# Token-to-channel turns by transfers of 32-partition squares and full-width transposes, and weight parts made 2048 elements at a time, in a float32 hybrid decoder layer

## The chip, the cores and the metric

The kernel runs on one core of one Trainium2 chip, in one launch. The metric is device time in microseconds (us). Engines: PE is TensorE (matmul), PEld its weight load, DVE is VectorE, ACT is ScalarE, POOL is GpSimd, SP is SyncE, which here only issues transfers. "Partition" is one of the 128 rows of on-chip memory.

## The reference

One decoder layer on x [256 tokens, 2048 channels], all float32, and a final norm:

```
h    = rmsnorm(x, ln1_w)
proj = h @ w_in          # q | k | v | pool input | z | x,B,C | dt | 3 gates: 13856 columns
att  = sliding-window attention with sinks      (1024 wide)
pool = trailing means over 2, 4, 8, 16 tokens minus the token, a map per group, a scale (1024)
ssm  = Mamba-2 SSD with conv, then y * silu(z) under a norm per group of 512   (2048)
merged = sum over the branches of sigmoid(gate_b) * (branch_b @ w_b)
x    = x + merged @ w_out
h2   = rmsnorm(x, ln2_w)
x    = x + (silu(h2 @ Wg) * (h2 @ Wu)) @ w_down     # feed-forward, 5632 wide
out  = rmsnorm(x, final_w)
```

## The kernel before, in words

Every large product is made of float32 numbers split in two parts of the type float32r, a = hi + lo, and takes three matmuls (hi hi, hi lo, lo hi; `three`, L180 to L184) into one accumulator. Weights stream from HBM in pieces of [128, n, columns], at most 2048 elements a partition, that is 1 MB: `weights` (L144) has SP load a piece into one of four `raw` buffers, and then, for each half of the piece, has ACT copy the high part into a `whi` buffer and DVE subtract it into a `wlo` buffer (`split`, L138 and L139; five buffers of 1024 elements of each). `tokens_block` (L186) is [256 tokens, up to 512 columns] = a^T W, with one accumulator per 128 tokens; `channels_block` (L210) is the product with channels on partitions. A piece of 512 columns is 24 matmuls.

The stages, in order: v and dt as x comes in; k and q; the convolutions and the attention between them; the SSD scan; the attention branch; pooling and its branch; z with the group norm of the SSD output; the SSD branch; the output projection; the feed-forward in three parts of 4, 4 and 3 blocks of 512 columns, each part's down projection behind it.

A product contracts over channels, so its left side must have channels on partitions, while a `tokens_block` leaves tokens on partitions. `turn` (L305) makes the change for a block [128 tokens, 2, 512 channels]: 16 DVE transposes (L314), each of one 32 by 32 square position over a tile of 32 partitions and 256 elements, in two groups of eight; then ACT and DVE split the result (L316 to L322; where a weight of the norm goes in, in four pieces with a scale per partition). It is used for 4 blocks of y (SSD output), 4 of m (merged), 4 of x2 (the residual) and 11 of ff (feed-forward).

Small work such as this is put in a list (`later`, `pause`) and taken from it by `side` (L122), one task for each half piece of a large product, with a share of DVE's time counted (SHARE, 1.4 us for a half piece of 1024 elements, capped at 4.0). That gives the order in which the program is written; the framework then plans each engine's own order of instructions from it by when it expects data and buffers. An engine runs its instructions in that planned order and waits at the first whose input is missing. Each transfer is queued on the engine that issues it: SP has the weights, x, the norm weights and the output; POOL has the small vectors at the start (L253, L355 to L359) and, later, a few additions (L638, L661, L703, L740).

Tiles of 4 KB a partition (`k4`) share 22 buffers.

Of the kernel before, what the change touches and what calls it, by code (L numbers as in the profile page):

```python
# [16 lines left out]
P = 128  # L17
D = 2048
# [25 lines left out]
SHARE = 1.4 / 1024  # of the vector engine's time per column of weights, for small work  # L44
# [3 lines left out]
# the constants' array: an identity, then the rest by column  # L48
# [8 lines left out]
def constants():  # L57
    c = np.zeros((P, K_N), np.float32)
    r = np.arange(P)
    c[:, K_LE:K_LE + P] = r[:, None] <= r[None, :]  # L60
    c[:, K_GT:K_GT + P] = r[:, None] > r[None, :]
    # a query's row: the previous block's keys, then its own block's
    c[:, K_MC:K_MC + P] = np.where(r[None, :] > r[:, None], 0.0, NEG)
    c[:, K_MP:K_MP + P] = np.where(r[None, :] <= r[:, None], 0.0, NEG)
    for g, w in enumerate(POOL_WINDOWS):
        n = np.minimum(np.arange(PADW) + 1, w).astype(np.float32)
        c[:, K_IV + g * PADW:K_IV + (g + 1) * PADW] = np.float32(1.0) / n
    return np.concatenate([np.eye(P, dtype=np.float32), c], axis=1)
# [3 lines left out]
def hybrid_block(ctx: ExitStack, tc: tile.TileContext, ins, out):  # L72
# [39 lines left out]
    # a task and its time on the vector engine, which is shared out over the pieces  # L112
# [22 lines left out]
    def split(src, hi, lo, scale=None):  # L135
        """src (SBUF or PSUM), times a scalar per partition, into its parts."""
        if scale is None:
            act.copy(hi, src)  # L138
            dve.tensor_tensor(lo, src, hi.bitcast(F32), ALU.subtract)  # L139
        else:  # L140
            act.activation(hi, src, AF.Copy, scale=scale)  # L141
            dve.scalar_tensor_tensor(lo, src, scale, hi.bitcast(F32), ALU.mult, ALU.subtract)

    def weights(loads, shape):  # L144
        """A piece of weights [128, n, cols], n * cols <= 2048: pairs of parts, each of half of n."""
        raw = wpool.tile([P, *shape], F32, tag="raw", name="raw", bufs=4)
        for to, src in loads:
            sp.dma_start(to(raw), src)
        n, cols = shape
        parts = []  # L150
        for h in range(2):
            a, b = h * (n // 2), (h + 1) * (n // 2)
            hi = wpool.tile([P, b - a, cols], F32R, tag="whi", name="whi", bufs=5)
            lo = wpool.tile([P, b - a, cols], F32R, tag="wlo", name="wlo", bufs=5)
            split(raw[:, a:b], hi, lo)
            parts.append((a, b, hi, lo))
        return parts
# [3 lines left out]

    class Parts:
        """An activation, channels on partitions: [128, channel tiles, 256 tokens] in two parts."""
# [16 lines left out]
    def three(o, xh, xl, yh, yl, first, last):  # L180
        """o (+)= x^T y without the product of the two low parts."""
# [4 lines left out]
    def tokens_block(a, nk, loads_of, cols, loaded=None):  # L186
        """[tokens, cols] = a^T W over nk channel tiles: one accumulator per 128 tokens."""
        accs = [acc() for _ in range(T)]
        step = 8 if cols <= 256 else 4
        for i in range(0, nk, step):  # L190
            n = min(step, nk - i)
            pieces = weights(loads_of(i, n), [n, cols])
            if loaded is not None:
                loaded(i)
            for s, e, hi, lo in pieces:
                for t in range(T):
                    tok = slice(t * P, (t + 1) * P)
                    for j in range(e - s):
                        k = i + s + j
# [9 lines left out]

    def channels_block(a, loads_of):  # L210
        """[256 channels, tokens] = W^T a over all of D: one accumulator per 128 channels."""
        accs = [acc() for _ in range(2)]
        for i in range(0, KD, 8):
            for s, e, hi, lo in weights(loads_of(i), [8, 256]):
                for j in range(e - s):
                    k = i + s + j
# [16 lines left out]
    def keep_warm(n):  # L233
        """Work for the tensor engine while it waits, so that its clock is up when the data comes."""
# [11 lines left out]
    for name, n in (("ln2_w", 16), ("ssm_norm_w", 16), ("pool_scale", 8), ("conv_b", 24)):  # L246
        VEC[name] = r0, n
        r0 += n
# [10 lines left out]
    # the engine's table, before its time  # L259
# [15 lines left out]
    def rsqrt(ss, n, shape, name, more=EPS):  # L275
        """(ss / n + more) ** -0.5: the engine's root, then a Newton step."""
# [11 lines left out]
    def transposed(block, k0, dst, scale=None):  # L288
        """block [128 tokens, 2, 512 channels] into dst's channel tiles k0..k0+3."""
# [15 lines left out]
    def turn(block, k0, dst, scale=None):  # L305
        """As transposed, by the vector engine's 32 by 32 squares: in three steps."""
        tt = k4([4, SEQ], F32, "tt")
        src = block.rearrange("p t (k j c) -> p t k j c", k=4, j=4)
        to = tt.rearrange("p k (t i s) -> p t k i s", t=T, i=4)

        def squares(rows_):
            for i in rows_:
                for j in range(4):
                    dve.transpose(to[32 * j:32 * j + 32, :, :, i, :], src[32 * i:32 * i + 32, :, :, j, :])  # L314

        def parts():  # L316
            if scale is None:
# [6 lines left out]
        later(lambda: squares((0, 1)), 2.0)  # L324
        later(lambda: squares((2, 3)), 2.0)
        later(parts, 1.2)

# [25 lines left out]
    for name in ("ln2_w", "ssm_norm_w", "pool_scale", "conv_b"):  # L353
        vec_load(name)
    pool.dma_start(vec[:96, 1, :], ins["conv_w"][0].rearrange("k (a c) -> (k a) c", c=P))  # L355
# [27 lines left out]
    # the factors as a row, on every partition  # L383
# [16 lines left out]
    # softplus(x) = max(x, 0) + 2 atanh(e / (2 + e)), e = exp(-|x|)  # L400
# [35 lines left out]
    def times_sums():  # L436
        # sums over a chunk: up to a token (second chunk), and behind it (first chunk)
# [19 lines left out]
    # ---- q and k: heads on partitions, a pair by tile; a key head in both halves of its tile  # L457
# [17 lines left out]
    def att_scores(j):  # L475
        for n in range(T):
# [6 lines left out]
            # the heads of one half of the partitions to a bank  # L483
# [73 lines left out]
    def conv(a, ci, dst):  # L557
        """Causal convolution and SiLU of a channel tile: a [128, 256] in PSUM."""
# [18 lines left out]
    # decay, and the product of C and B, by chunk and group  # L577
# [15 lines left out]
    def mix_product(c, g):  # L593
        """[s, 8 heads, l]: (C_l . B_s) exp(sum over s < t <= l of dt a), zero for s > l."""
# [15 lines left out]
    # B of the first chunk, tokens on partitions  # L610
# [22 lines left out]
    def ssd_x(c, g):  # L633
# [3 lines left out]
        # the skip term, in place  # L637
# [56 lines left out]
    def branch(br, j, a_parts, w, sg):  # L694
# [3 lines left out]
        for t, a in enumerate(tokens_block(a_parts, nk, plain_loads(w, 0, j * NB, NB), NB)):  # L698
# [15 lines left out]
    po = Parts(8, "po")  # L714

    def pool_mix(pair):
# [3 lines left out]
        for (g, mhi, mlo), (_, _, wh, wl) in zip(pair, w2):  # L720
# [44 lines left out]
    ssg = tiny([T, GROUPS], "ssg", 1)  # L765
    ssm = Parts(KD, "ssm")
    for g in range(GROUPS):
# [13 lines left out]
        turn(ys[g], 4 * g, ssm, lambda k: vcol("ssm_norm_w", k))  # L781
# [3 lines left out]
    for j in range(4):  # L785
# [7 lines left out]
        elif j > 1:  # L793
            turn(m4[j], 4 * j, mp)

# [8 lines left out]
    for j in range(4):  # L804
        for t, a in enumerate(tokens_block(mp, KD, plain_loads(ins["w_out"][0], 0, j * NB, NB), NB)):
# [3 lines left out]
        turn(x2[j], 4 * j, x2p, lambda k: vcol("ln2_w", k))  # L809
# [11 lines left out]
    def down(j, c0, cols, i, accs):  # L821
        """A block's sums into the residual; where i is given, they are whole."""
# [11 lines left out]
    for some in FF_PARTS:  # L834
        f = Parts(4 * len(some), "f")
        for i, b in enumerate(some):
            a_ = k4([T, NB], F32, "ff")
            for t, a in enumerate(tokens_block(x2p, KD, plain_loads(wgu, 0, b * NB, NB), NB)):
                act.activation(a_[:, t, :], a, AF.Silu, scale=rstd2[:, t:t + 1])
            if b == FB - 1:  # L840
                # the root's table, before its time
                act.activation(tiny([1], "junk1"), a_[:, 1, :1], AF.Square)
                act.activation(tiny([1], "junk1"), rstd2[:, :1], AF.Sqrt)
            for t, a in enumerate(tokens_block(x2p, KD, plain_loads(wgu, 0, DFF + b * NB, NB), NB)):
# [3 lines left out]
            turn(a_, 4 * i, f)  # L848
        k0, nk = 4 * some[0], 4 * len(some)
        last = some[-1] == FB - 1  # L850
        for j in range(3 if last else 4):
            down(j, 0, NB, j if last else None, tokens_block(f, nk, plain_loads(wd, k0, j * NB, NB), NB))
    down(3, 0, 256, 3, tokens_block(f, nk, plain_loads(wd, k0, 3 * NB, 256), 256))

# [1 line left out]
    wl = []  # L856
    for i in range(0, nk, 8):
        n = min(8, nk - i)
        raw = wpool.tile([P, n, 256], F32, tag="raw", name="raw", bufs=4)
        sp.dma_start(raw, rows(wd, k0 + i, n, 3 * NB + 256, 256))  # L860
# [55 lines left out]
```

## Time and profile before

| | |
|---|---|
| median of 3 runs | 1677.84 us (1677.47 to 1678.03) |
| span of the profiled execution, first to last instruction | 1675.7 us |
| that execution's time outside its span | not shown; the median lies 2.1 us above the span |
| PE, PEld busy | 1660.0 us (99%), 1417.6 us (85%) |
| DVE, ACT, POOL busy | 1145.6 us (68%), 792.7 us (47%), 61.1 us (4%) |
| moved by DMA | 312.5 MB, 184468 packets, 187 GB/s in the mean |

A timeline row has start (us from the span's first instruction), duration in us, engine, line of the kernel, operation, output<-inputs, shape, count, and in brackets the engine's idle time before it and what ended that. Matmuls overlap: a row of 0.39 us may be followed by the next 0.23 us later, so starts are compared, not durations. A row of groups has the busy us and the mean ns of one instruction behind the first bar, and the idle time before them behind the second.

### The profile page before, as it was taken

What the parts mean: (1) busy time and instruction counts of PE and PEld (TensorE: products, weight loads), DVE (VectorE), ACT (ScalarE), POOL (GpSimd) and SP (SyncE); (2) the same over time, 40 slices, a digit from 0 to 9 for tenths busy, and PEclk for the clock granted to TensorE, in tenths of its full rate; (3) what the DMA queues carried; (4) which work ended last, traced back from release to release, by engine and by line L of the source; (5) the groups of instructions that cost most, each with busy time, mean ns of one, the idle gap of its engine ahead of it and who ended that gap; (6) DMA issues with size and microseconds to landing.
All of it is one profiled execution on the core that took longest, in us unless ns stands there. A gap on an engine that the chain in (4) does not pass through costs nothing.

```text
span 1675.7 us, 21335 instructions
## 1 busy us (share of the span) xinstructions
PE 1660.0 (99%) x8511; PEld 1417.6 (85%) x8511; DVE 1145.6 (68%) x1577; ACT 792.7 (47%) x970; POOL 61.1 (4%) x53
## 2 busy tenths in 40 slices
PE   9999999999999999999999999999999999999997
PEld 8999998888988888888788888888888888888887
DVE  7688788885654469945798866665456666546675
ACT  6357555444444457644445544443344444344443
POOL 1000001110220000000000000000000000000000
PEclk9999999999999999999999999999999999999999
DMA  9544454455566555566475565556565556555552
GB/s 295 183 150 155 153 191 151 151 165 163 160 218 200 185 193 193 185 202 199 152 250 185 178 211 185 195 201 212 191 200 192 187 199 197 186 194 201 186 178 88
DMA packets 184468, 312.53 MB, mean 187 GB/s; under 512 B 7388, under 2 KB 57824, under 8 KB 184368
## 3 DMA queue, kind: packets, MB, share of 16 engines
q1 hardware_dynamic: 183856, 310.67, 56.5%
q8 instruction: 66, 1.08, 0.3%
q0 software_dynamic: 368, 0.43, 0.1%
q14 instruction: 34, 0.28, 0.0%
q10 hardware_dynamic: 144, 0.07, 0.0%
HBM read 309.05 MB, written 2.10 MB: 186 GB/s over the span
## 4 chain that ended last, share of the span: by engine, by line
PE 93%; DVE 4%; ACT 1%; DMA 1%; issue 1%; SPq 0%; DVEq 0%; ACTq 0%
PE acc L184 30%; PE acc L182 30%; PE acc L183 30%; DVE wlo L139 1%; DVE tt L314 1%; PE sm L644 1%; DMA x<-in_x_dram 1%; PE tr L489 1%; ACT whi L138 0%; DVE cv L565 0%; PE sm L604 0%; PE sm L532 0%; PE tr L521 0%; DVE y L631 0%; PE sm L651 0%
## 5 line engine op out<-in xcount | busy, mean ns | idle before, releaser
L139 DVE TENSOR_TENSOR wlo<-raw,whi 128x1024 fp32r<-128x1024 f32 (+2 forms) x582 | 705.4, 1227 | 454.3 <-ACT whi L138 453.1
L138 ACT CAST whi<-raw 128x1024 fp32r<-128x1024 f32 (+2 forms) x582 | 603.6, 1040 | 741.4 <-PE acc L184 622.5
L183 PE MATMUL acc<-wlo,x2p_hi 128*128 128x512 f32 x704 | 274.0, 389 | 0.0
L184 PE MATMUL acc<-whi,x2p_lo 128*128 128x512 f32 x704 | 274.0, 389 | 0.0
L182 PE MATMUL acc<-whi,x2p_hi 128*128 128x512 f32 x704 | 274.0, 389 | 0.0
L182 PE MATMUL acc<-whi,h_hi 128*128 128x512 f32 (+1 forms) x544 | 212.7, 392 | 1.0 <-ACT h_hi L141 1.0
L183 PE MATMUL acc<-wlo,h_hi 128*128 128x512 f32 (+1 forms) x544 | 208.8, 384 | 0.3 <-DVE wlo L139 0.3
L184 PE MATMUL acc<-whi,h_lo 128*128 128x512 f32 (+1 forms) x544 | 208.7, 385 | 0.3
L182 PE MATMUL acc<-h_hi,whi 128*128 128x256 f32 x672 | 191.6, 285 | 0.0
L184 PE MATMUL acc<-h_hi,wlo 128*128 128x256 f32 x672 | 190.7, 284 | 0.0
L183 PE MATMUL acc<-h_lo,whi 128*128 128x256 f32 x672 | 190.7, 284 | 0.0
L183 PEld LDWEIGHTS acc<-wlo,x2p_hi 128*128 128x128 f32 x704 | 132.2, 188 | 27.4
L184 PEld LDWEIGHTS acc<-whi,x2p_lo 128*128 128x128 f32 x704 | 132.2, 188 | 27.4
L182 PEld LDWEIGHTS acc<-whi,x2p_hi 128*128 128x128 f32 x704 | 132.2, 188 | 27.4
L184 PE MATMUL acc<-whi,f_lo 128*128 128x512 f32 (+1 forms) x352 | 134.6, 382 | 0.4 <-DVE f_lo L139 0.4
L182 PE MATMUL acc<-whi,f_hi 128*128 128x512 f32 (+1 forms) x352 | 134.5, 382 | 0.0
L183 PE MATMUL acc<-wlo,f_hi 128*128 128x512 f32 (+1 forms) x352 | 134.5, 382 | 0.0
L182 PEld LDWEIGHTS acc<-h_hi,whi 128*128 128x128 f32 x672 | 128.9, 192 | 2.1 <-issue 1.5
L184 PEld LDWEIGHTS acc<-h_hi,wlo 128*128 128x128 f32 x672 | 128.9, 192 | 1.4 <-issue 1.3
L183 PEld LDWEIGHTS acc<-h_lo,whi 128*128 128x128 f32 x672 | 128.9, 192 | 0.4 <-issue 0.3
L182 PEld LDWEIGHTS acc<-whi,h_hi 128*128 128x128 f32 x544 | 102.1, 188 | 23.2 <-issue 1.9
L183 PEld LDWEIGHTS acc<-wlo,h_hi 128*128 128x128 f32 x544 | 102.2, 188 | 22.2 <-issue 1.9
(236 smaller groups left out, 1898.5 us busy)
## 6 DMA issues: line engine op xcount, KB each, us to landing
raw<-in_w_in_dram SPq DMA_DIRECT2D x106, 1024.0 KB, 5.2
raw<-in_w_gate_up_dram SPq DMA_DIRECT2D x88, 1024.0 KB, 5.1
raw<-in_w_down_dram SPq DMA_DIRECT2D x43, 1024.0 KB, 5.2
raw<-in_w_ssm_br_dram SPq DMA_DIRECT2D x16, 1024.0 KB, 5.2
raw<-in_w_out_dram SPq DMA_DIRECT2D x16, 1024.0 KB, 5.9
raw<-in_w_attn_br_dram SPq DMA_DIRECT2D x8, 1024.0 KB, 5.1
raw<-in_w_pool_br_dram SPq DMA_DIRECT2D x8, 1024.0 KB, 5.1
x<-in_x_dram SPq DMA_DIRECT2D x8, 512.0 KB, 7.8
```

The lines of the kernel that those rows point to most:

```text
L138: act.copy(hi, src)
L139: dve.tensor_tensor(lo, src, hi.bitcast(F32), ALU.subtract)
L182: pe.matmul(o, lhsT=xh, rhs=yh, start=first, stop=False)
L183: pe.matmul(o, lhsT=xh, rhs=yl, start=False, stop=False)
L184: pe.matmul(o, lhsT=xl, rhs=yh, start=False, stop=last)
L314: dve.transpose(to[32 * j:32 * j + 32, :, :, i, :], src[32 * i:32 * i + 32, :, :, j, :])
L489: pe.matmul(p[:, i * w:(i + 1) * w], lhsT=qT[2 * j + i][half, n * P:(n + 1) * P], rhs=kT[j][half, keys], start=True, stop=True,)
L644: pe.matmul(p[:, i * HD:(i + 1) * HD], lhsT=mt[:, i, :], rhs=xdt[:, i, :], start=True, stop=True)
```

## The change

`turn` sends the block's 16 squares of 32 partitions (32 tokens, all of the two token blocks, 128 channels; 32 KB each) by 16 transfers from SBUF to SBUF into a new tile `mid`, and then makes two DVE transposes over all 128 partitions and 512 elements. The transfers are queued on POOL, or, for the last turn before its consumer (`soon`: m of the last branch block, x2 of the last block, the last ff block of each feed-forward part), on POOL, SP and ACT in rotation (6, 5, 5). The task list has the move, then a pause of 6.0 us (3.0 if soon) and then the transposes and the split in one task of 2.6. In the turned tile, partition p has channels 4p to 4p+3 of a block of 512, where it had p, p+128, p+256, p+384: so the weights of the products that read turned tiles (w_ssm_br, w_out, w_gate_up, w_down) are loaded in the matching order (`turned`, four neighbouring rows to a partition; packets as long as before), and the norm weights ln2_w and ssm_norm_w come as a [128, 4, 4] tile by two POOL transfers of runs of 4 elements, instead of rows that PE turns.

`weights` splits a whole piece at once: one ACT copy and one DVE subtraction of 2048 elements instead of two of 1024. `raw` has 3 buffers instead of 4; `whi` and `wlo` have 3 of 2048 elements instead of 5 of 1024. Comments are left out in the new file.

```diff
     def weights(loads, shape):
-        raw = wpool.tile([P, *shape], F32, tag="raw", name="raw", bufs=4)
+        raw = wpool.tile([P, *shape], F32, tag="raw", name="raw", bufs=3)
         for to, src in loads:
             sp.dma_start(to(raw), src)
-        n, cols = shape
-        parts = []
-        for h in range(2):
-            a, b = h * (n // 2), (h + 1) * (n // 2)
-            hi = wpool.tile([P, b - a, cols], F32R, tag="whi", name="whi", bufs=5)
-            lo = wpool.tile([P, b - a, cols], F32R, tag="wlo", name="wlo", bufs=5)
-            split(raw[:, a:b], hi, lo)
-            parts.append((a, b, hi, lo))
-        return parts
+        hi = wpool.tile([P, *shape], F32R, tag="whi", name="whi", bufs=3)
+        lo = wpool.tile([P, *shape], F32R, tag="wlo", name="wlo", bufs=3)
+        split(raw, hi, lo)
+        return hi, lo
+    def turned(w, k0, n, c0, cols):
+        return [
+            ((lambda r, b=b: r[:, b:b + 4, :]),
+             w[(k0 + b) * P:(k0 + b + 4) * P, c0:c0 + cols].rearrange("(p k) c -> p k c", k=4))
+            for b in range(0, n, 4)
+        ]
...
-    def turn(block, k0, dst, scale=None):
-        tt = k4([4, SEQ], F32, "tt")
-        src = block.rearrange("p t (k j c) -> p t k j c", k=4, j=4)
-        to = tt.rearrange("p k (t i s) -> p t k i s", t=T, i=4)
-        def squares(rows_):
-            for i in rows_:
-                for j in range(4):
-                    dve.transpose(to[32 * j:32 * j + 32, :, :, i, :], src[32 * i:32 * i + 32, :, :, j, :])
+    def turn(block, k0, dst, scale=None, soon=False):
+        mid = k4([T, 4, P], F32, "mid")
+        queues = (pool, sp, act) if soon else (pool,)
+        def move():
+            for n in range(16):
+                i, j = n // 4, n % 4
+                queues[n % len(queues)].dma_start(
+                    mid[32 * j:32 * j + 32, :, i, :], block[32 * i:32 * i + 32, :, j * P:(j + 1) * P]
+                )
         def parts():
+            tt = k4([4, SEQ], F32, "tt")
+            for t in range(T):
+                dve.transpose(
+                    tt.rearrange("p k (t i s) -> p t i k s", t=T, i=4)[:, t],
+                    mid[:, t].rearrange("p i (c k) -> p i k c", k=4),
+                )
...
-        later(lambda: squares((0, 1)), 2.0)
-        later(lambda: squares((2, 3)), 2.0)
-        later(parts, 1.2)
+        later(move)
+        pause(3.0 if soon else 6.0)
+        later(parts, 2.6)
...
-    for name in ("ln2_w", "ssm_norm_w", "pool_scale", "conv_b"):
+    for name in ("pool_scale", "conv_b"):
         vec_load(name)
+    vec_t = const.tile([P, 2, KD // 4, 4], F32, name="vec_t")
+    for i, name in enumerate(("ln2_w", "ssm_norm_w")):
+        pool.dma_start(vec_t[:, i], ins[name][0].rearrange("(b p k) -> p b k", p=P, k=4))
...
-            turn(m4[j], 4 * j, mp)
+            turn(m4[j], 4 * j, mp, soon=j == 3)
...
-        turn(x2[j], 4 * j, x2p, lambda k: vcol("ln2_w", k))
+        turn(x2[j], 4 * j, x2p, lambda k: tcol(0, k), soon=j == 3)
...
-            turn(a_, 4 * i, f)
+            turn(a_, 4 * i, f, soon=i == len(some) - 1)
```

## Rows read from the trace of the kernel before

**Rows 1.** The page: busy time of each engine, and the chain by engine

```profile
PE 1660.0 (99%) x8511; PEld 1417.6 (85%) x8511; DVE 1145.6 (68%) x1577; ACT 792.7 (47%) x970; POOL 61.1 (4%) x53
...
PE 93%; DVE 4%; ACT 1%; DMA 1%; issue 1%; SPq 0%; DVEq 0%; ACTq 0%
```

**Rows 2.** Stretches: busy us and instructions of each engine, PEclk, DMA share, GB/s

```profile
0.00:40.00 40.00, 36.44 (x247) 34.11 (x248) 28.07 (x66) 27.19 (x49) 5.85 (x15) 1.00 1.00 307
...
90.00:190.00 100.00, 99.72 (x799) 92.71 (x798) 82.74 (x151) 64.50 (x136) 0.00 (x0) 1.00 0.49 154
190.00:240.00 50.00, 49.24 (x407) 48.78 (x407) 46.63 (x74) 27.99 (x37) 2.44 (x2) 1.00 0.52 164
...
820.00:840.00 20.00, 17.90 (x73) 14.32 (x72) 19.46 (x29) 8.59 (x9) 1.07 (x1) 0.91 0.46 148
...
1050.00:1600.00 550.00, 550.00 (x2429) 455.57 (x2428) 329.84 (x372) 232.91 (x231) 0.00 (x0) 1.00 0.59 195
1600.00:1640.00 40.00, 39.58 (x175) 32.44 (x174) 31.41 (x46) 19.53 (x25) 0.00 (x0) 1.00 0.53 172
```

**Rows 3.** Timeline of PE, 826 to 836 us

```profile
828.94 0.39 PE L182 MATMUL acc<-whi,ssm_hi 128*128 128x512 f32 x1
831.43 0.50 PE L183 MATMUL acc<-wlo,ssm_hi 128*128 128x512 f32 x1 [2.10 <-DVE wlo L139]
...
835.65 0.39 PE L182 MATMUL acc<-whi,ssm_hi 128*128 128x512 f32 x1
```

**Rows 4.** Timeline of DVE, 770 to 850 us

```profile
812.33 7.17 DVE L314 STREAM_TRANSPOSE tt<-m 32x256 f32<-32x256 f32 x16
...
822.94 7.18 DVE L314 STREAM_TRANSPOSE tt<-m 32x256 f32<-32x256 f32 x16
```

**Rows 5.** Groups of DVE by line and shape

```profile
L139 DVE TENSOR_TENSOR wlo<-raw,whi 128x1024 fp32r<-128x1024 f32 x568 | 695.5, 1239 | 449.7 <-ACT whi L138 448.6
L314 DVE STREAM_TRANSPOSE tt<-ff 32x256 f32<-32x256 f32 x176 | 76.7, 436 | 2.6
...
L139 DVE TENSOR_TENSOR wlo<-raw,whi 128x512 fp32r<-128x512 f32 x6 | 4.0, 688 | 3.9 <-ACT whi L138 3.9
```

**Rows 6.** Groups of ACT by line and shape

```profile
L138 ACT CAST whi<-raw 128x1024 fp32r<-128x1024 f32 x568 | 594.7, 1050 | 735.9 <-PE acc L184 620.5 <-PE acc L183 90.2 <-DVE wlo L139 10.2
...
L138 ACT CAST whi<-raw 128x576 fp32r<-128x576 f32 x8 | 5.3, 670 | 0.1
```

**Rows 7.** Timeline of DVE, 1250 to 1264 us

```profile
1251.54 1.40 DVE L845 SCALAR_TENSOR_TENSOR ff<-acc,rs_r,ff 128x512 f32<-128x512 f32 x2
1252.98 7.18 DVE L314 STREAM_TRANSPOSE tt<-ff 32x256 f32<-32x256 f32 x16
```

**Rows 8.** Groups of POOL

```profile
L357 POOL DMA_DIRECT2D heads<-in_d_skip_dram x1 | 0.5, 547 | 0.0
L358 POOL DMA_DIRECT2D sink<-in_attn_sink_dram x1 | 0.5, 539 | 1.2 <-DMA vec<-in_ln_w_dram 1.2
```

**Rows 9.** Transfers: issues, size, median us to landing

```profile
raw<-in_w_gate_up_dram SPq DMA_DIRECT2D x88, 1024.0 KB, 5.1
...
out_dram<-x SPq DMA_DIRECT2D x8, 256.0 KB, 2.6
...
cst<-in_cst_dram POOLq DMA_DIRECT2D x1, 288.0 KB, 6.5
```

**Rows 10.** Timeline of DVE, then of PE, 1599 to 1613 us

```profile
1601.14 7.19 DVE L314 STREAM_TRANSPOSE tt<-ff 32x256 f32<-32x256 f32 x16
...
1611.91 0.50 PE L184 MATMUL acc<-whi,f_lo 128*128 128x512 f32 x1 [0.42 <-DVE f_lo L139]
```

**Rows 11.** Timeline of PE, from the start

```profile
9.87 0.53 PE L182 MATMUL acc<-whi,h_hi 128*128 128x288 f32 x2
```

**Rows 12.** Timeline of DVE, then of PE, 196 to 262 us

```profile
212.83 4.63 DVE L139 TENSOR_TENSOR wlo<-raw,whi 128x1024 fp32r<-128x1024 f32 x4
...
214.84 0.28 PE L184 MATMUL acc<-h_hi,wlo 128*128 128x256 f32 x1
```

More of the change, by code (lines that the diff above doesn't have):

```diff
@@ L191, in tokens_block @@
             n = min(step, nk - i)
-            pieces = weights(loads_of(i, n), [n, cols])
+            hi, lo = weights(loads_of(i, n), [n, cols])
             if loaded is not None:
                 loaded(i)
-            for s, e, hi, lo in pieces:
+            for s, e in ((0, n // 2), (n // 2, n)):
                 for t in range(T):
                     tok = slice(t * P, (t + 1) * P)
-                    for j in range(e - s):
-                        k = i + s + j
+                    for j in range(s, e):
+                        k = i + j
                         three(
@@ L208, in plain_loads, with turned_loads @@
         return lambda i, n: [(lambda r: r[:, :, :], rows(w, k0 + i, n, c0, cols))]
+    def turned_loads(w, k0, c0, cols):
+        return lambda i, n: turned(w, k0 + i, n, c0, cols)
     def channels_block(a, loads_of):
@@ L213, in channels_block @@
         for i in range(0, KD, 8):
-            for s, e, hi, lo in weights(loads_of(i), [8, 256]):
-                for j in range(e - s):
-                    k = i + s + j
+            hi, lo = weights(loads_of(i), [8, 256])
+            for s, e in ((0, 4), (4, 8)):
+                for j in range(s, e):
+                    k = i + j
                     for c in range(2):
@@ L245, in hybrid_block @@
     VEC = {}
-    for name, n in (("ln2_w", 16), ("ssm_norm_w", 16), ("pool_scale", 8), ("conv_b", 24)):
+    for name, n in (("pool_scale", 8), ("conv_b", 24)):
         VEC[name] = r0, n
@@ L351, in hybrid_block, with tcol @@
     rst = const.tile([P, SEQ], F32, name="rst")
-    for name in ("ln2_w", "ssm_norm_w", "pool_scale", "conv_b"):
+    for name in ("pool_scale", "conv_b"):
         vec_load(name)
+    vec_t = const.tile([P, 2, KD // 4, 4], F32, name="vec_t")
+    for i, name in enumerate(("ln2_w", "ssm_norm_w")):
+        pool.dma_start(vec_t[:, i], ins[name][0].rearrange("(b p k) -> p b k", p=P, k=4))
+    def tcol(i, k):
+        return vec_t[:, i, k // 4, k % 4:k % 4 + 1]
     pool.dma_start(vec[:96, 1, :], ins["conv_w"][0].rearrange("k (a c) -> (k a) c", c=P))
@@ L697, in branch @@
         nk = w.shape[0] // P
-        for t, a in enumerate(tokens_block(a_parts, nk, plain_loads(w, 0, j * NB, NB), NB)):
+        loads = turned_loads if br == 2 else plain_loads
+        for t, a in enumerate(tokens_block(a_parts, nk, loads(w, 0, j * NB, NB), NB)):
             if br == 0:
@@ L719, in pool_mix @@
         w2 = weights([(lambda r: r[:, :, :], pw[:, 2 * g0:2 * g0 + 4])], [4, 256])
-        for (g, mhi, mlo), (_, _, wh, wl) in zip(pair, w2):
+        for i, (g, mhi, mlo) in enumerate(pair):
+            wh, wl = (w[:, 2 * i:2 * i + 2] for w in w2)
             p = sm().rearrange("p (k s) -> p k s", k=2)
@@ L780, in hybrid_block @@
         later(finish, 1.5)
-        turn(ys[g], 4 * g, ssm, lambda k: vcol("ssm_norm_w", k))
+        turn(ys[g], 4 * g, ssm, lambda k: tcol(1, k))
     sg_ssm = [gate(2, j) for j in range(2)]
@@ L804, in hybrid_block @@
     for j in range(4):
-        for t, a in enumerate(tokens_block(mp, KD, plain_loads(ins["w_out"][0], 0, j * NB, NB), NB)):
+        for t, a in enumerate(tokens_block(mp, KD, turned_loads(ins["w_out"][0], 0, j * NB, NB), NB)):
             dve.tensor_tensor(x2[j][:, t, :], a, x2[j][:, t, :], ALU.add)
@@ L837, in hybrid_block @@
             a_ = k4([T, NB], F32, "ff")
-            for t, a in enumerate(tokens_block(x2p, KD, plain_loads(wgu, 0, b * NB, NB), NB)):
+            for t, a in enumerate(tokens_block(x2p, KD, turned_loads(wgu, 0, b * NB, NB), NB)):
                 act.activation(a_[:, t, :], a, AF.Silu, scale=rstd2[:, t:t + 1])
@@ L843, in hybrid_block @@
                 act.activation(tiny([1], "junk1"), rstd2[:, :1], AF.Sqrt)
-            for t, a in enumerate(tokens_block(x2p, KD, plain_loads(wgu, 0, DFF + b * NB, NB), NB)):
+            for t, a in enumerate(tokens_block(x2p, KD, turned_loads(wgu, 0, DFF + b * NB, NB), NB)):
                 dve.scalar_tensor_tensor(
@@ L851, in hybrid_block @@
         for j in range(3 if last else 4):
-            down(j, 0, NB, j if last else None, tokens_block(f, nk, plain_loads(wd, k0, j * NB, NB), NB))
-    down(3, 0, 256, 3, tokens_block(f, nk, plain_loads(wd, k0, 3 * NB, 256), 256))
+            down(j, 0, NB, j if last else None, tokens_block(f, nk, turned_loads(wd, k0, j * NB, NB), NB))
+    down(3, 0, 256, 3, tokens_block(f, nk, turned_loads(wd, k0, 3 * NB, 256), 256))
     wl = []
@@ L858, in hybrid_block @@
         n = min(8, nk - i)
-        raw = wpool.tile([P, n, 256], F32, tag="raw", name="raw", bufs=4)
-        sp.dma_start(raw, rows(wd, k0 + i, n, 3 * NB + 256, 256))
+        raw = wpool.tile([P, n, 256], F32, tag="raw", name="raw", bufs=3)
+        for to, src in turned(wd, k0 + i, n, 3 * NB + 256, 256):
+            sp.dma_start(to(raw), src)
         for b in range(0, n, 4):
```

## The prediction

> **What bounds the kernel now.** I read the page first: PE is busy 1660.0 of 1675.7 us, DVE 1145.6, ACT 792.7, POOL 61.1, and the chain that ended last is PE for 93% and DVE for 4% [rows 1]. That doesn't yet say that PE can't be fed better, so I read PE's busy time stretch by stretch: from 1050 to 1600 us it has 550.00 of 550.00 [rows 2], 2429 matmuls at 0.2264 us each. There no work taken off DVE or ACT can be worth anything. What is lost elsewhere is little [rows 2]: 3.56 us in the first 40, 0.28 from 90 to 190, 0.76 from 190 to 240, 2.10 from 820 to 840, 0.42 from 1600 to 1640. The change adds and removes no large matmul, so it lives within these few microseconds on the good side, and on the bad side in what it can make PE wait for.
>
> The one real hole is at 828.9 us: PE waits 2.10 us for a `wlo` [rows 3], and the granted clock of 820 to 840 is 0.91 where it is 1.00 in the other stretches [rows 2]. From 828.94 to 835.65 there are twelve starts; at 0.2264 us they take 2.72, so 4.0 us are lost there, wait and lower clock (1.2 instead of 2.4 GHz for part of it) together. The cause stands in DVE's timeline: two turns of m behind each other, 7.17 and 7.18 us of squares [rows 4], with hardly a weight subtraction between.
>
> **The change part by part.**
>
> *Squares on DVE go.* 23 turns of 16 transposes at 436 ns [rows 5] are 160.4 us of DVE. In their place come 46 transposes of 512 elements. None is in the trace; the nearest row is a subtraction of 512 elements, 688 ns [rows 5], so 0.70 each, 32 us in all (at twice that, 64). DVE loses about 128 us. In the feed-forward that is worth nothing: DVE goes away for 1.40 + 7.18 us at a turn [rows 7] and PE still has 550.00 of 550.00. At 828.9 it removes the cause: two turns then hold DVE for about 2.8 us of transposes, not 14.4. I take the 4.0 us as gained. What is late next there is the squares' landing, which nothing needs for more than a block.
>
> *The transfers.* A turn has 16 of 32 KB. POOL issues one in 0.547 us, and its ninth at the start of the kernel waited 1.2 us for the landing of its first [rows 8]: eight in flight. Landing takes between 2.6 us (256 KB out) and 6.5 us (a POOL transfer while the DMA engines were full) [rows 9]. With 18 turns on POOL alone: the last square issues at 8 x 0.547 + the wait + 8 x 0.547, so at 8.75 to 11.4 us after the block is done, and lands at 11 to 18. Those blocks are wanted 20 us or more later (a further block of 16 channel tiles is 96 matmuls, 21.7 us), so PE pays nothing as long as DVE does not stand waiting (the first rival). In all 12.1 MB more go over engines that are 59% busy in the long stretch [rows 2], 3.9% on 312.5 MB: hidden; if that cover were gone it would be the weights' landing, 5.1 us [rows 9], that grows, against 16.3 us which three `raw` buffers allow.
>
> The Trainium skill speaks against such transfers: DMA: Bandwidth & Descriptors, Anatomy of one DMA and Rules for kernel authors, gives each about 2.0 us fixed and says that below 64 KB one pays mostly overhead. One after the other the sixteen would by an estimate from that page take 33 us a turn. The trace has POOL issue the next before the last has landed [rows 8], so I keep 11 to 18.
>
> *The soon turns.* Five turns put 6 on POOL, 5 each on SP and ACT: 6 x 0.547 + 2.6 to 6.5 = 5.9 to 9.8 us, then 1.4 of transposes, so 7.3 to 11.2 where squares took 7.2. Behind come, as before, a high and a low part (1.05 and 1.24 us, [rows 5, 6]). Four of the five are wanted in the fourth piece of their consumer, 72 matmuls or 16.3 us after the block: 11 to 15 us is in time. The last feed-forward part has three blocks, its third piece comes at 10.9 us, and there the old turn was already late: 7.19 us of squares and a wait of PE for f_lo of 0.42 [rows 10]. The new one is 0.1 to 4.0 later unless PE is given other matmuls first. I take +1.0, ends -0.4 and +4.0. SP's own five stand in front of weight loads and wait for the block; the weights in `raw` cover that, and ACT's five cost it some 2 us of its slack.
>
> *Whole pieces.* 284 pairs of splits become single ones. By the slope between 512 and 1024 elements [rows 5] DVE takes 2.34 us instead of 2.48, by 576 and 1024 [rows 6] ACT 1.92 instead of 2.10: 40 and 51 us less in all, hidden under PE. But the first half of a piece is ready (2.34 - 1.24) + (1.92 - 1.05) = 2.0 us later, and buffers come free by the piece. So DVE may be away less long: 8.6 us cost nothing before [rows 7], about 6.6 after. Where DVE is the tight engine that shows. From 190 to 240 us it is busy 46.6 of 50 [rows 2]; at 212.83 it makes four halves in a row, each done within 1.2 us, and PE takes the first at 214.84 [rows 12]. As a whole piece it is done at about 215.2: 0.3 late, likewise for its neighbours. I take +0.5, ends -0.8 (the stretch's idle time goes) and +3. From 90 to 190 (DVE 82.7 of 100) I take 0, ends -0.3 and +2.
>
> *The start.* PE begins the products at 9.87 us [rows 11], behind a split of 576 elements, now 1152: 0.5 us later on ACT (0.67 to 1.16 by the slope), 0.6 on DVE. The DMA engines are full there, 1.00 over 40 us at 307 GB/s [rows 2]. The third `raw` buffer as the last leaves 576 KB of weights behind x, 1.9 us earlier at that rate; the two norm weights come in 1024 runs of 16 bytes, not shown in the trace, between 0 and, at the mean price of a packet (195 GB/s at 0.59 busy and 1.7 KB make 82 ns), 5.3 us on 16 engines. A packet a hundredth as long should be near the low end. I take +0.6 for all of it, ends -1.9 and +6.
>
> *The sum*, against the profiled span of 1675.7: -4.0 + 1.0 + 0.5 + 0 + 0.6 = -1.9, so 1673.8; the median of the runs lies 2.1 above the span, so **1675.9 us**. A median tells 0.2% from no change, 3.4 us here, so this is no change.
>
> **The rivals.**
>
> *A. DVE waits for the squares (slower).* DVE runs its list in order; behind the transposes stand the next weight subtractions, and PE waits for those. The point that decides is 6.6 us of standing, as above. The pause of 6.0 is 3 to 5 half pieces of 2.7 us, 8 to 14 us after the move; squares that land at 11 to 18 let DVE stand 0 to 10. For it: the landing while weights stream is not in the trace. Against it: the planner places the transposes by when it expects `mid`. Standing 7.9 us costs 1.3 at each of 18 turns: +23, some 1699 us. On the same side the Trainium skill (SBUF — State Buffer, Two separate sides) has POOL unable to write a transfer's descriptors while DVE runs a two-port operation; no run here shows it.
>
> *B. Whole pieces starve PE wherever DVE is tight (slower).* Four attention heads and four SSD groups at 1 us each beside the sum's +0.5: -1.9 + 7.5, 1683.4. For it [rows 12]; against it the stretch has only 0.76 us idle, and DVE gains 0.14 a piece.
>
> *C. The hole at 828.9 stays*, because ACT and DVE still take two turns there at once, or the landing is in the way: -1.9 + 4.0, 1679.9. So the change wouldn't do what it says for the time. Against it: 14.4 us of squares are the whole cause.
>
> *D. All holes close*: -4.0 - 0.4 - 0.8 - 0.3 - 1.0 at the start, 1671.3. For it: planner and DVE have more room everywhere. Against it: the 2.0 us of later halves.
>
> **How the numbers follow.** The sum's case has 0.55 (own range 1673 to 1679), C 0.13, D 0.12, A 0.08, B 0.12. Of the sum's 0.55 the part below 1674.5 (gain over 0.2%) is 0.23, with D 0.35 faster; the rest and C are 0.45 within 0.2%; A and B are 0.20 slower. The range runs from 1671.5 (D) to 1686 (past B), leaving out A and the edges.
>
> **What would show it.** Right: PE busy all of 820 to 840 at clock 1.00; DVE's busy time near 978 us, ACT's near 742, POOL's near 235 (318 issues of 0.547); 46 transposes near 0.70 us; no wait of DVE for `mid` over 6 us. Wrong: PE waiting for `wlo` behind a DVE that waits for a transfer (A), or in many places between 90 and 400 us (B); first products well after 10.5 us; PE waiting for f_hi or f_lo of the last part by more than 4 us.

## The result, and the profile after

The changed kernel takes 1688.59 us (median of 4 runs, 1688.1 to 1691.4) beside 1677.65 of the kernel before (4 runs, 1675.75 to 1678.03): ratio of the runs' means 1.0071, 95% interval 1.0058 to 1.0083. It is slower by 0.7%. The forecast was 1675.9, no change, with a range from 1671.5 to 1686: wrong, the measured time lies above the range.

The page after, to hold beside [rows 1]: DVE has lost 152 us, ACT 53, and the span has grown from 1675.7 to 1686.7. The chain of the page is followed back only to 897.9 us here (its shares add up to 46%, before to 100%), so the two rows can't be set side by side share by share. In the part that it covers, transfers (`mid`) and the DVE work behind them stand between the stretches of PE at x2 and in the last feed-forward part.

```profile
PE 1663.3 (99%) x8511; PEld 1417.0 (84%) x8511; DVE 993.7 (59%) x964; ACT 739.6 (44%) x679; POOL 221.1 (13%) x371
...
PE 41%; DMA 2%; DVE 2%; issue 1%; POOL 0%; ACTq 0%; DVEq 0%; ACT 0%
```

PE's part of the stretches (PE busy, instructions, granted clock, DMA share, GB/s), beside [rows 2]. Two more of the kernel before, then those after:

```profile
640.00:730.00 90.00, 90.00 (x399) 1.00 0.62 209
840.00:1050.00 210.00, 210.00 (x928) 1.00 0.58 202
```

```profile
0.00:40.00 40.00, 35.29 (x237) 1.00 0.90 270
...
190.00:240.00 50.00, 49.68 (x410) 1.00 0.53 165
640.00:730.00 90.00, 86.68 (x372) 0.98 0.59 187
820.00:840.00 20.00, 20.00 (x90) 1.00 0.63 205
840.00:1050.00 210.00, 205.25 (x899) 1.00 0.67 216
1050.00:1600.00 550.00, 550.00 (x2428) 1.00 0.62 202
1600.00:1640.00 40.00, 37.85 (x160) 0.96 0.56 181
```

The hole at 820 to 840 has closed, as forecast. Two stretches that were full are no longer full, 640 to 730 (z, with the turns of y) and 840 to 1050 (output projection, with those of x2), and the last part has lost more. To count the low clock as well as the waits I take the starts of PE's matmuls against the usual pitch of their shape (gaps over 60 ns): 0 to 40 us loses 9.0 (before 7.9), 640 to 740 5.85 (0), 820 to 840 0 (3.9), 860 to 980 6.3 (0), 1600 to 1640 4.1 (0.7), 180 to 240 1.6 (1.95). Over the whole span that is 12.2 more, and the span is 11.0 longer; of the difference 0.5 is a shorter tail behind the last matmul.

What DVE waits for tells why (us in total, times, longest), and then what PE waits for most:

```profile
DVE tt L329 <- DMA mid<-ff: 60.5, 11, 6.8
DVE tt L329 <- DMA mid<-y: 28.9, 4, 8.1
DVE tt L329 <- DMA mid<-x: 24.1, 4, 8.1
```

```profile
PE acc L186 <- DVE wlo L139: 8.8, 7, 1.9
```

I call a wait of an engine in the midst of its list a stand. One by one, the stands are 5.4, 7.6, 8.1 and 7.8 us at y, 8.1, 8.0, 7.5 and 0.5 at x2, up to 5.0 at m and 3.9 to 6.8 at ff. Behind the six of 7.5 to 8.1, PE loses 0.4 to 3.8 us each by the starts, and 1.9 behind the last turn of x2.

One of the six, at y, first on POOL, then on DVE, on ACT and on PE:

```profile
678.95 6.31 POOL L322 DMA_DIRECT2D mid<-y  x12 [14.51 <-ACT whi L138]
687.25 2.10 POOL L322 DMA_DIRECT2D mid<-y  x4 [1.99 <-DMA mid<-y]
```

```profile
691.74 2.06 DVE L329 STREAM_TRANSPOSE tt<-mid 128x512 f32<-128x512 f32 x2 [8.14 <-DMA mid<-y]
693.71 2.26 DVE L139 TENSOR_TENSOR wlo<-raw,whi 128x2048 fp32r<-128x2048 f32 x1
```

```profile
693.83 1.71 ACT L141 ACTIVATE ssm_hi<-tt,vec_t 128x256 fp32r<-128x256 f32 x4 [8.21 <-DVE tt L329]
```

```profile
693.73 0.39 PE L185 MATMUL acc<-whi,h_hi 128*128 128x512 f32 x1
696.03 0.50 PE L186 MATMUL acc<-wlo,h_hi 128*128 128x512 f32 x1 [1.91 <-DVE wlo L139]
...
697.39 0.63 PE L187 MATMUL acc<-whi,h_lo 128*128 128x512 f32 x1
697.82 0.63 PE L185 MATMUL acc<-whi,h_hi 128*128 128x512 f32 x1
```

POOL begins to issue the sixteen squares at 678.95 and ends at 689.35: 8.4 us of issuing, and 1.99 us of wait for a landing. DVE is done at 683.6 with all that stands ahead of the transposes in its list, and stands for 8.14 us; ACT, which needs the turned tile for its high part, stands for 8.21. The weight subtraction behind them starts at 693.71, PE wants its result at 694.1 and waits 1.91 us; afterwards it runs at the lower clock for a while (0.43 us from start to start; the granted clock of 696.5 to 700.3 us is 0.55).

The new instructions, by group, and the landing of a square of y:

```profile
L329 DVE STREAM_TRANSPOSE tt<-mid 128x512 f32<-128x512 f32 x46 | 47.5, 1070 | 119.6 <-DMA mid<-ff 60.5 <-DMA mid<-y 28.9 <-DMA mid<-x 24.1
```

```profile
L322 POOL DMA_DIRECT2D mid<-ff x146 | 76.8, 535 | 573.9 <-DVE ff L869 561.5
```

```profile
mid<-y POOLq DMA_DIRECT2D x48, 32.0 KB, 4.4
```

POOL's 0.535 us an issue is what [rows 8] gave. The transposes take 1.07 us, where I had 0.70 from [rows 5].

The last part, DVE and then PE, beside [rows 10]:

```profile
1616.69 2.06 DVE L329 STREAM_TRANSPOSE tt<-mid 128x512 f32<-128x512 f32 x2 [4.06 <-DMA mid<-ff]
1618.67 2.26 DVE L139 TENSOR_TENSOR wlo<-raw,whi 128x2048 fp32r<-128x2048 f32 x1
1620.84 1.23 DVE L139 TENSOR_TENSOR f_lo<-tt,f_hi 128x1024 fp32r<-128x1024 f32 x1
```

```profile
1619.89 0.50 PE L185 MATMUL acc<-whi,f_hi 128*128 128x512 f32 x1 [0.65 <-ACT f_hi L138]
...
1622.12 0.79 PE L187 MATMUL acc<-whi,f_lo 128*128 128x512 f32 x1 [1.50 <-DVE f_lo L139]
```

The block is done at 1609.1, its squares have landed by 1616.7, and PE waits for f_hi and then for f_lo.

### The profile page after: what moved, and what is told of

Its sections match the earlier page's. It is cut to its first block, busy times and chain, and to the rows that moved or that the text cites. A ratio compares the mean times of both kernels' runs of the same rounds, so it can differ in the third digit from the quotient of the medians.

```text
span 1686.7 us, 20724 instructions
## 1 busy us (share of the span) xinstructions
PE 1663.3 (99%) x8511; PEld 1417.0 (84%) x8511; DVE 993.7 (59%) x964; ACT 739.6 (44%) x679; POOL 221.1 (13%) x371
## 5 line engine op out<-in xcount | busy, mean ns | idle before, releaser
L139 DVE TENSOR_TENSOR wlo<-raw,whi 128x2048 fp32r<-128x2048 f32 (+2 forms) x291 | 660.8, 2273 | 468.3 <-ACT whi L138 467.2
L138 ACT CAST whi<-raw 128x2048 fp32r<-128x2048 f32 (+2 forms) x291 | 549.4, 1889 | 649.9 <-PE acc L187 529.1
L322 POOL DMA_DIRECT2D mid<-ff x146 | 76.8, 535 | 573.9 <-DVE ff L869 561.5
```

The source lines that it names most:

```text
L322: queues[n % len(queues)].dma_start(mid[32 * j:32 * j + 32, :, i, :], block[32 * i:32 * i + 32, :, j * P:(j + 1) * P])
```

## The experiments

Theory 1: DVE runs its list in order, reaches the transposes before the squares have landed, and the weight subtractions behind them come late. Theory 2: pieces of 2048 elements are too coarse by themselves. Theory 3: the transfers take DMA time from the weights.

**Transposes later (e1_late).** The place of the transposes in DVE's list is the framework's, which plans it by when it expects `mid`. Here they are tied to a later weight subtraction instead (a longer pause alone was not run):

```diff
-        later(move); pause(6.0); later(parts, 2.6)
+        # y, and x2 of the first three blocks
+        later(lambda: (move(), due.append((len(made) + 5, parts)))); pause(8.6)
...
+            with tc.issue_after(made[-1].ins):      # made: the weight subtractions so far
                 dve.transpose(...)                  # weights() runs what is due
```

> The changed kernel, but the transposes of the y turns and of the first three x2 turns are put on DVE one to two weight subtractions later (behind a named subtraction), so that DVE reaches them after the squares have landed. All else is as in the changed kernel. Theory 1 (DVE stands in its order waiting for squares, up to 8.1 us, and the weight subtractions behind it come late): the stands of 7.5 to 8.1 us at y and x2 go, PE is busy 90 of 90 in 640 to 730 us and within 0.5 us of all of 840 to 1050, and of the 12.1 us lost there (5.85 + 6.3) 10 to 12 come back: 1688.6 becomes 1676.5 to 1679. Theory 2 (the pieces of 2048 elements come too late by themselves, with scalings and evacuations piled on them): the subtractions are as long as before, so most of the loss stays, 1685 to 1689. Theory 3 (contention of the transfers with weight loads): nothing changes, 1687 to 1690.

1676.43 us (10 runs), ratio to before 0.9996 (0.9987 to 1.0006). Waits of DVE for `mid`, and PE's stretches:

```profile
DVE tt L334 <- DMA mid<-ff: 59.8, 11, 6.5
...
DVE tt L334 <- DMA mid<-y: 2.2, 1, 2.2
```

```profile
640.00:730.00 90.00, 90.00 (x399) 1.00 0.66 215
...
840.00:1050.00 210.00, 209.19 (x921) 1.00 0.68 220
```

The stands at y are down to one of 2.2 us, those at x2 are gone, and 12 us are back with every instruction, transfer and piece size as it was. Theory 1 holds; 2 and 3 can't explain that. PE loses nothing behind the last turn of x2 either, which was not edited, so its 1.9 us hung on the stands ahead of it. The high parts that ACT makes of the turned tiles come later with the transposes, so that this run alone doesn't part DVE's stand from ACT's; PE's waits in the changed kernel are for DVE's `wlo` (8.8 us) and hardly for ACT's `whi` (0.7). The stands at ff, of up to 6.5 us, cost nothing.

**Half pieces again (e2_half).**

```diff
-        hi = wpool.tile([P, *shape], ..., bufs=3); lo = ...; split(raw, hi, lo)
+        for a, b in ((0, n // 2), (n // 2, n)):
+            hi = wpool.tile([P, b - a, cols], ..., bufs=5); lo = ...
+            split(raw[:, a:b], hi, lo)
```

> The changed kernel with the weight parts made by half pieces again (1024 elements, four raw buffers, five of each part), the turns by transfers kept. Theory 1: DVE stands as long (7.5 to 8.1 us), but a half piece bears 8.6 us of absence where a whole one bears 6.6, so about 2.0 us are taken off each of some seven stands that cost 1.5 to 2.0: 4 to 12 us come back, and 1.0 at the start: 1676 to 1684. Theory 2 (granularity alone): all of it comes back, with the hole at 828.9 closed the kernel is faster than the one before: 1673 to 1676. Theory 3 (contention): 1687 to 1690.

1698.2 us, ratio 1.0125 (1.011 to 1.014): all three missed. DVE's waits, ACT's timeline, and PE's waits from 640 to 1050 us:

```profile
DVE tt L332 <- DMA mid<-y: 26.1, 4, 7.9
DVE tt L332 <- DMA mid<-x: 25.2, 3, 9.3
```

```profile
718.48 1.71 ACT L141 ACTIVATE ssm_hi<-tt,vec_t 128x256 fp32r<-128x256 f32 x4 [10.36 <-DVE tt L332]
...
722.66 4.84 ACT L138 CAST whi<-raw 128x1024 fp32r<-128x1024 f32 x5
```

```profile
PE acc L190 <- DVE wlo L139: 8.3, 9, 1.5
PE acc L189 <- ACT whi L138: 4.8, 3, 2.7
```

ACT stands too, in its own order, as in the changed kernel (8.21 us at the turn of y above), but longer: the high part of the turn waits for DVE's transposes, 10.36 us, with the next weight copies behind it. And five halves are 2.5 pieces of weights made ahead (60 matmuls, 13.6 us of PE), where three whole buffers are 72 matmuls, 16.3 us. At y the stands are no longer than in the changed kernel, and by the starts PE loses 8.7 us there where it lost 5.85: so halves bear less, and that is shown; for which of these reasons is argued. At x2 two of the stands are longer themselves (9.3 and 9.0 us), so the loss there doesn't compare.

**Whole pieces alone (e3_whole).** The kernel before with that half of the change only:

```diff
-        for h in range(2): ... bufs=5 ... split(raw[:, a:b], hi, lo)
+        hi = wpool.tile([P, *shape], ..., bufs=3); lo = ...; split(raw, hi, lo)
```

> The kernel before with one part of the change alone: whole pieces of 2048 elements (three raw buffers, three of each part); turns by DVE squares as before. Theory 2 (granularity): slower by most of what the changed kernel loses, 1685 to 1692, with PE waits for wlo in 640 to 730 and 840 to 1050 us. Theory 1 (standing for squares): no squares to wait for; 7.2 us of squares in two runs of 3.6 are little above the 6.6 us that whole pieces bear, so +1.0 at the start, +1 to +3 at the hole at 828.9 and up to 2 elsewhere: 1679 to 1683.

1684.66 us, ratio 1.0047 (1.0031 to 1.0064): just under theory 2's 1685, above theory 1's 1683. DVE, and PE's stretches:

```profile
673.62 7.18 DVE L310 STREAM_TRANSPOSE tt<-y 32x256 f32<-32x256 f32 x16
680.84 2.29 DVE L139 TENSOR_TENSOR wlo<-raw,whi 128x2048 fp32r<-128x2048 f32 x1
```

```profile
640.00:730.00 90.00, 87.28 (x383) 1.00 0.58 197
...
840.00:1050.00 210.00, 206.13 (x907) 1.00 0.57 199
```

With squares on DVE, whole pieces (with their numbers of buffers) do cost: behind 7.18 us of squares a subtraction of 2.29 us has to be done before PE can go on, where it was one of 1.24 [rows 5], and PE waits 1.12 us for this one. So each part of the change alone is slower (squares kept 1684.66, halves kept 1698.2), and both together are not the sum of the two.

**The read order of the transposes (e6_plainsrc).** The order of DVE's instructions is that of the changed kernel; the channels come out in an order that doesn't match the weights' rows.

```diff
-                    mid[:, t].rearrange("p i (c k) -> p i k c", k=4),
+                    mid[:, t].rearrange("p i (k c) -> p i k c", k=4),
```

> The changed kernel, whose transposes read the squares' 128 channels as four runs of 32 neighbouring elements and not as 32 elements at a stride of four; the channels then come out in another order than the weights' rows, which is the part of the computation that it changes. If the 1.07 us of a transpose (0.70 predicted) come from the stride: near 0.70 to 0.80, and DVE 12 to 17 us less busy, the time 1686 to 1689 since DVE's standing stays. If from the operation itself: 1.0 to 1.1 again.

1680.21 us in one run, 1677.23 of the kernel before beside it. DVE's group, its waits, and PE's stretches:

```profile
L329 DVE STREAM_TRANSPOSE tt<-mid 128x512 f32<-128x512 f32 x46 | 30.1, 691 | 118.7 <-DMA mid<-ff 60.3 <-DMA mid<-y 27.9 <-DMA mid<-x 23.2
```

```profile
DVE tt L329 <- DMA mid<-y: 27.9, 4, 8.2
DVE tt L329 <- DMA mid<-x: 23.2, 3, 8.0
```

```profile
640.00:730.00 90.00, 88.57 (x389) 1.00 0.62 200
...
840.00:1050.00 210.00, 207.10 (x910) 1.00 0.67 219
```

691 ns instead of 1070: the stride is the difference, and 0.691 is the 0.70 that I had taken from a row of 512 neighbouring elements. The stands are as long as before (8.2 and 8.0 us), yet this one run is 8.4 us below the change's median, against an expected 1686 to 1689: missed. Its trace agrees: by the starts PE loses 3.6 less at y, 2.2 less from 860 to 980 and 2.2 less in the last part. Two transposes are 0.76 us shorter at every turn, which at the six long stands and in the last part makes 5.3 of these 8; some 3 are the lower clock, which this trace doesn't have behind its waits.

The Trainium skill has a rule for this (SBUF — State Buffer, Door 1: The DMA port swizzle): SBUF has lines of 16 bytes, and each access that crosses to a new line pays a penalty. A stride of four float32 goes to a new line each time, and the trace agrees: 1070 ns against 691. The same note calls strides free up to four float32; with a stride of just four elements the trace does not bear that out.

**The last part (e5_pair).** The first two down blocks take turns, so that the third piece comes after 21.7 us and not 10.9; its transposes are tied behind that part's third subtraction.

```diff
-        for j in range(3): down(j, ..., tokens_block(f, nk, ...))
+        for j, i in ((0, 0), (0, 4), (1, 0), (1, 4), (0, 8), (1, 8)):
+            hi, lo = weights(turned(wd, k0 + i, 4, j * NB, NB), [4, NB])
...
+            if i == 8: down(j, 0, NB, j, accs[j])
```

> The changed kernel, in whose last feed-forward part the first two blocks of the down projection are taken in turn: pieces 0 and 1 of both, then piece 2 of both, so that the last turn is wanted 21.7 us behind its block and not 10.9; its transposes stand behind the weight subtraction of the third piece. If the wait for f_hi and f_lo of 2.2 us and the low clock behind it are what the last part loses (4.1 us over the pitch): 1684.3 to 1685.3, and PE busy all of 1600 to 1640. If the wait only goes to another place (the two blocks' evacuation, the last loads): 1687 to 1689.

1685.62 us (4 runs, 1684.13 to 1689.21), ratio 1.0055 (1.004 to 1.007); 3.0 less than the change, expected 3.3 to 4.3. By this time alone the gain isn't clear of the change's interval; the stretch shows it:

```profile
1600.00:1640.00 40.00, 40.00 (x179) 1.00 0.63 206
```

By the starts the last part loses 0 where it lost 4.1. The execution profiled is the slowest of the four, and from 860 to 980 us, where nothing was edited, it loses 11.4 us, where the changed kernel's loses 6.3: behind two of its waits the clock is at the lower level, behind none of the changed kernel's there. What a stand costs thus varies by some microseconds from run to run.

**All turns over three queues (e4_queues).**

```diff
-        queues = (pool, sp, act) if soon else (pool,)
+        queues = (pool, sp, act)
```

> The changed kernel with every turn's transfers on POOL, SP and ACT in rotation, not only the soon ones; the order of the transposes as the framework plans it. Theory 1 (POOL's one queue makes the squares late: 16 issues of 0.53 us and a wait for the ninth): they land some 7.5 us behind the block, as the soon turns' did, and not 12.8, so stands of 8 become about 3 and the waits of PE at y and x2 go: 1677 to 1681. Rival (each issue on SP and ACT costs about 1 us there, 5 a turn, and ACT stands in order too): the weight copies come late in their place, 1686 to 1696.

1688.55 us, ratio 1.0071 (1.0058 to 1.0085): no gain. PE's stretches, and ACT's timeline behind a branch block:

```profile
640.00:730.00 90.00, 90.00 (x399) 1.00 0.66 216
...
840.00:1050.00 210.00, 201.51 (x864) 0.98 0.66 215
```

```profile
845.09 3.76 ACTq L322 DMA_DIRECT2D mid<-m  x5
848.98 1.91 ACT L138 CAST whi<-raw 128x2048 fp32r<-128x2048 f32 x1 [9.71 <-DMA mid<-m]
```

At y the stands fell to 5.7 us at most and PE is busy 90 of 90: there POOL's single queue was the cause of the late squares. At m and x2 the issuing engines stand themselves: ACT is idle 9.71 us before its next weight copy, waiting for the block and then, for 3.76 us, issuing five squares. DVE's stands there are up to 8.5 (m) and 9.9 us (x2), and by the starts PE loses 5.6 us from 840 to 860 and 8.7 from 860 to 980. Both ends of the expectation are seen, in different stretches, and they cancel.

**Both repairs (e7_both), and three variants of it.** e7_both is e1_late's and e5_pair's edits in one kernel.

> The changed kernel with both repairs: the y and the first three x2 transposes later on DVE (as in e1_late) and the down projection of the last part by two blocks in turn (as in e5_pair). If the two losses are separate places: 1676.4 (e1_late) less 3 to 4, so 1672.4 to 1673.5, which is 3 to 4 us under the kernel before, with PE busy 550 of 550 and 40 of 40 in the last two stretches. If the loss only moves to the next place: 1675 to 1677.

1672.89 us (10 runs), ratio 0.9977 (0.9968 to 0.9986): the losses were separate, 3.5 us below e1_late, and the kernel is 0.2% faster than the one before.

```profile
640.00:730.00 90.00, 90.00 (x399) 1.00 0.66 215
...
840.00:1050.00 210.00, 209.54 (x925) 1.00 0.67 220
...
1600.00:1640.00 40.00, 40.00 (x178) 1.00 0.60 193
```

e9_vec also takes the norm weights' two transfers out of the start:

```diff
-    for i, name in enumerate(("ln2_w", "ssm_norm_w")): pool.dma_start(vec_t[:, i], ...)
+        with tc.issue_after(skip.ins):              # the scan's first POOL addition
+            for i, name in enumerate(("ln2_w", "ssm_norm_w")): pool.dma_start(vec_t[:, i], ...)
```

> e7_both, with the two transfers of the norm weights in runs of 16 bytes taken out of the start and issued behind the first POOL addition of the scan. If these runs cost the start (whole pieces without them, e3_whole, had 36.0 us of PE busy in the first 40, with them 34.3 to 35.3): 1 to 1.5 us less than e7_both, PE busy about 36 in 0 to 40. If the start's loss is the first whole piece: no difference to e7_both within 0.5 us.

1672.65 us, ratio 0.9976 (0.9967 to 0.9986): no difference. e11_start adds to that two split instructions for each of the first four pieces:

```diff
-        made.append(split(raw, hi, lo))
+        for a, b in ((0, n // 2), (n // 2, n)) if shape[1] == 288 else ((0, n),):
+            last = split(raw[:, a:b], hi[:, a:b], lo[:, a:b])
+        made.append(last)
```

> e9_vec with the four first pieces (288 columns) split by two instructions of 576 elements each on ACT and on DVE, into the same whole buffers. If the start waits for the first whole split: 0.5 to 1.5 us less than e9_vec (1672.65). If what the start waits for is the order in which DMA brings x and the weights: within 0.5 us of it.

1672.74 us, ratio 0.9975 (0.9965 to 0.9985): no difference either. What the start lost, about 1 us, stays open; it is not these runs of 16 bytes, and nothing shows that it is the first split.

e8_half is e7_both with e2_half's pieces.

> e7_both with half pieces (1024 elements). If halves were slower with transfers (e2_half, 1698.2) only because the stands come on top of them: with no stand longer than 3 us at y and x2 it is within 1.5 us of e7_both. If halves are worse by themselves (2.5 pieces of parts ready instead of 3, more instructions on ACT): 4 us or more above e7_both.

1676.49 us, ratio 0.9999 (0.999 to 1.0008): 3.6 above e7_both, between the two expectations. By the starts it loses 4.7 us at one turn of m, 860 to 900 us, where e7_both loses 0.7; at y, x2 and ff neither loses any. That place is a stand too: DVE waits 6.8 us for the squares of a turn of m there, where in e7_both it waits 0.6 at that turn and 5.9 at the next. So most of e2_half's loss was the stands, and what is left of the halves' own part is one place, in an order that the framework planned otherwise.

**The hole without transfers (e12_early).** The kernel before, one thing else:

```diff
-        if j == 1:
-            mp = Parts(KD, "mp")
-            for i in range(2): turn(m4[i], 4 * i, mp)
-        elif j > 1:
-            turn(m4[j], 4 * j, mp)
+        if j == 0:
+            mp = Parts(KD, "mp")
+        turn(m4[j], 4 * j, mp)
```

> The kernel before, with squares and half pieces as they are, and one thing else: the turn of m's first block is queued behind the first SSD branch block and that of the second behind the second, not both behind the second. If the hole at 828.9 us comes from two turns of squares behind each other: it closes, 20.00 of 20 from 820 to 840, and 1677 becomes 1672.5 to 1674. If squares of 7.2 us cost there by themselves, on top of the branch's additions: 1676 to 1680, with a wait for wlo at each turn.

1673.69 us (11 runs), ratio 0.9979 (0.997 to 0.9988).

```profile
820.00:840.00 20.00, 20.00 (x90) 1.00 0.64 211
```

Two turns of squares behind each other were the whole cause of the hole [rows 3, 4], and a change of a few lines mends it; what the full change gained there could be had without it. e7_both and e12_early can't be told apart by their intervals.

## Why the prediction was wrong

*The step that failed* is the wait that the part on the transfers put at nothing: "PE pays nothing as long as DVE does not stand waiting". The sum has no term for the stand; it was left to rival A at a chance of 0.08. The landing was right: POOL issues for 10.4 us and the last square has landed 12.8 us behind the first issue, inside my 11 to 18. What I didn't do was to ask where in DVE's list the transposes would be. I let "the planner places the transposes by when it expects `mid`" speak against the rival; the order it made has them ahead of the landing by 7.5 to 8.1 us at six of the eight turns of y and x2. e1_late shows what that costs: with the transposes later, the 5.85 us at y and the 6.1 at x2 are gone.

*The decision point of rival A* was about right and its price was not. I had 6.6 us of standing, and 1.3 at each of 18 turns. Stands of up to 6.8 at ff cost nothing (550.00 of 550.00), those of 7.5 to 8.1 cost 0.4 to 2.1 us, one of them 3.8 with the lower clock behind it; so it was decided at six places and one behind them, not at eighteen. The better measure is the stand plus the transposes, DVE's whole absence from the weights: 8.9 is free at ff, 9.6 to 10.2 is not at y and x2. It is no sharp edge for all stages: in e6_plainsrc 8.8 costs 0.8 us at x2. The last turn of m, which I had in time, is at the edge as well: it loses 0.2 us, and in e1_late's trace 1.4, most of it a wait of PE for that turn's low part.

*The transposes*, 0.70 each and free: mis-sized, 1.07, because they read at a stride of 16 bytes (e6_plainsrc). In DVE's sum that is 17 us of no account; behind the stands and in the last part it was worth some 8 us (one run). A term "hidden under PE" is free only up to the edge, and this one lay at it.

*The last feed-forward part*, +1.0 with ends -0.4 and +4.0: measured +3.4 by the starts. The landing of 7.5 us is inside my 5.9 to 9.8, but two transposes of 1.03 us and the subtraction of a whole piece (2.26 us) come between it and f_lo. e5_pair recovers it.

*Whole pieces*, +0.5 at 190 to 240: measured 0.44 less idle time there, and 90 to 190 has 0.11 less (99.83 busy); rival B did not happen. "DVE may be away less long" did not show as I put it: with the transfers, halves are worse (e2_half), and with the squares, whole ones are (e3_whole). I reckoned only with the first half's later end and left out that three whole buffers hold more than five halves; that this is the reason is argued.

*Right*: the hole closes (3.9 of 4.0); DMA traffic is hidden (landing of gate_up weights 5.5 us, [rows 9] 5.1; e1_late has all the transfers and not the loss); ff gains nothing; the busy time of ACT (739.6, forecast 742). POOL's came out at 221.1, forecast 235, with 0.535 us an issue. The five issues of a soon turn, put at some 2 us of ACT, held ACT's queue for 4.85 us at the last ff block; no run prices them by themselves. The start lost 1.0, forecast 0.6, for reasons that stay open.

The forecast's sum with the measured terms: -3.9 (hole) + 3.4 (last part) - 0.3 (180 to 240) + 1.0 (start) + 5.85 + 6.3 (y and x2, the 0.2 of m with them) = 12.35, for a span 11.0 longer. Without the stands it would have been 0.2. (Rival D comes to 1671.3 by its own sum, where the range that begins with it has 1671.5.)

## What to carry to other kernels

Moving work from an engine to transfers turns busy time into a wait in that engine's fixed order: before pricing that wait at nothing, find the place of the consumer in the order, and compare landing plus what follows with the parts that lie ready ahead, on each engine that stands (here ACT as well as DVE). Tie the consumer behind enough other work by an explicit order, or ask first whether a smaller reordering closes the hole. An instruction off the bottleneck is priced by its place: 0.38 us more on each of 46 transposes cost nothing at most of them and some 8 us at a few.

## What the runs showed of the hardware that I had not expected

- A DVE transpose of 128 x 512 float32 took 691 ns reading neighbouring elements and 1070 ns at a stride of 16 bytes.
- A POOL queue issued a transfer of 32 KB in 0.535 us and waited up to 2.0 us for landings within sixteen of them (at y behind the twelfth, at x2 behind the eighth). The Trainium skill's (DMA: Bandwidth & Descriptors, Anatomy of one DMA) about 2.0 us fixed per transfer is less than what this trace has beside the weight loads: 3.7 to 4.5 us in the median from POOL's issue to landing.
- After a wait of PE of 1.91 us the clock was at its lower level for some 3 us (0.43 us per matmul of 512 columns instead of 0.226), so that this wait cost 3.8 us, about twice itself. After one of 1.84 us, at 930 us in the same trace, it was not (granted clock 1.00 from 926 to 935).
